# A decoder block on one core: values projected with channels on partitions, and the router's logits and the closing norm rearranged

## The chip, the cores and the metric

One Trainium2 chip, of which the kernel uses one core. The metric is the device time of one execution, in microseconds (us); less is better. The kernel before takes 1893.37 us, the median of three runs (1891.93 to 1896.53).

## The reference, cut to what matters

The block is one decoder layer for 512 tokens of width 2048, in fp32:

```python
h    = rmsnorm(x) * (1 + sc_a) + sh_a
proj = h @ w_in                       # q_a k_a v_a | q_b k_b v_b f_b
o_a  = sliding_window_gqa(q_a, k_a, v_a)          # 16 query heads, 4 kv heads
o_b  = forgetting_attention(q_b, k_b, v_b, f_b)   # 16 heads of 64: v_b is 512 x 1024
x    = x + g_a * (concat(rmsnorm(o_a), rmsnorm(o_b)) @ w_out)
h2   = rmsnorm(x) * (1 + sc_m) + sh_m
logits = h2 @ [w_group | w_expert] + bias         # 4 + 32 columns
# top 1 of 4 groups, then top 2 of its 8 experts, each a SwiGLU of 2048 -> 512 -> 2048
x    = x + g_m * moe(h2, logits)
out  = rmsnorm(x) * final_g
```

"The second head group" is `o_b`; its values are `v_b = h @ w_in[:, 3584:4608]`. The change touches how `v_b` is made, how the 36 logits are made, and the last `rmsnorm`.

## The kernel before

TensorE (PE) does nearly all of the arithmetic. A product `PE.matmul(o, lhsT, rhs)` keeps `lhsT` (128 rows, up to 128 columns) in the array and streams the columns of `rhs` past it; its result has the columns of `lhsT` on partitions. Projections split each factor into a rounded part and a rest and sum three products (`mm3`, lines 213 to 216). A plain fp32 product shows as two records in the trace.

The stages follow one another: the modulation and the first projections (to about 172 us), attention (to about 735), the output projection (to about 890), the routing, and 32 experts in 16 pairs (from about 900). The order on every queue is the order in which the program is written; nothing is reordered.

**Attention.** `attend` (line 844) walks over twelve segments (counted from 0), each some units of softmax work (`a1` scores and softmax, `b` transposes of the probabilities, two units later, `c` the product with the values). Between them a `Fill` hands PE pieces of the projections that later segments need. A piece states its own length in us when it yields; `fill.take(step)` lets pieces run until their stated lengths add up to what was granted, and a segment's end drains what is left before the next segment begins. `FILLS` (line 374) says which pieces lie in which segment: the values `v_b` are 4 groups of 256 columns (4 heads), 8 pieces each, and the last pieces of the groups end segments 1, 4, 7 and 9. Beside it, `side` steps sum up the modulation vectors on VectorE (DVE), ScalarE (ACT) and GpSimd (POOL).

A group of values is made by `natural` (line 539): the tokens' activations are the stationary factor, 256 columns of weights stream, and the result has tokens on partitions, as the product with the probabilities wants it. That is 3 products for each of 16 pieces of depth and 4 blocks of 128 tokens, 192 to a group, 768 in all. ACT copies the four blocks from PSUM into `vbs[g]` (line 903). Queries and keys are made by `transposed` (line 521) the other way: weights stationary, all 512 tokens streamed, channels on partitions.

**Output projection.** Its 2048 columns are made in four chunks of 512 (`cc` in the order 2, 0, 1, 3). While PE makes the next chunk, a `Tail` finishes the one before: for each block `tb` of 128 tokens it transposes the new `x1` (`tr`) and multiplies it with the router's weights (`logit`, line 1129): 4 products whose stationary factor is the transposed `x1`, with 36 streamed columns. DVE adds the 128x36 result into `lg` (lines 1134 and 1136). For the last chunk the four results stay in PSUM (`lp4`), are added to `lg` (line 1199) and multiplied by the tokens' `rs` (line 1211).

**Routing.** A chain of some 30 small DVE instructions chooses the experts. Meanwhile `turn(n)` gives PE `n` idle 128-column products: 22 before the ranks `rk` (line 1257), 8 behind them.

**Experts and the end.** Weights stream in through a ring of tiles; the DMA queue SP waits for a tile until PE is done with it. The last pair's output is made in five chunks of columns. As each is added to the total (line 1446), `last_norm` (line 1599) has ACT square it into `sf5`. Behind the last, DVE sums the five columns (1608), scales (1609) and takes the root (`rsqrt_`), and then writes 8 halves of the output, each followed by its transfer (1616 and 1617).

Of the kernel before, what the change touches and what calls it, by code (L numbers as in the profile page):

```python
# [8 lines left out]
F32 = mybir.dt.float32  # L9
# [3 lines left out]
AF = mybir.ActivationFunctionType  # L13
OP = mybir.AluOpType
AX = mybir.AxisListType

T = 512
D = 2048
TB = 4
EPS = 1e-6  # L20
# [33 lines left out]
def kernel(  # L54
# [8 lines left out]
    V, S, G, PE, SP = nc.vector, nc.scalar, nc.gpsimd, nc.tensor, nc.sync  # L63
# [23 lines left out]
    sb = att.enter_context(tc.tile_pool(name="start", bufs=1))  # L87
# [11 lines left out]
    ident = big.tile([128, 128], F32, name="ident")  # L99
# [113 lines left out]
    def mm3(o, lhi, llo, rhi, rlo, first, last, **kw):  # L213
        PE.matmul(o, lhi, rhi, start=first, stop=False, **kw)  # L214
        PE.matmul(o, lhi, rlo, start=False, stop=False, **kw)  # L215
        PE.matmul(o, llo, rhi, start=False, stop=last, **kw)  # L216

    hT_hi = fr.tile([128, 4, 4, T], F32R, tag="B", name="hT_hi")
    hT_lo = [big.tile([128, 4 * n, T], F32R, tag=f"C{i}", name=f"hT_lo{i}") for i, n in enumerate((3, 1))]

    def kt(ts, k, sl=slice(0, T)):

        return ts[k // 12][:, k % 12, sl]

    def proj_T(accs, hi, lo, cc, j, jj, o=0):

        for i, a in enumerate(accs):
            sl = slice(o + i * 128, o + (i + 1) * 128)
            mm3(a, hi[:, jj, sl], lo[:, jj, sl], hT_hi[:, cc, j, :], kt(hT_lo, 4 * cc + j),
                cc == 0 and j == 0, cc == 3 and j == 3)  # L230
# [158 lines left out]
    ws = Stream(items)  # L389
# [54 lines left out]
    sb = att.enter_context(tc.tile_pool(name="att", bufs=1, reuse_waits="tile"))  # L444
# [63 lines left out]
    def bank(shape, name):  # L508

        return pb["pool"].tile(shape, F32, tag=pb["tag"], name=name, bufs=pb["bufs"])  # L510
# [3 lines left out]
    def accs(tag, name):  # L514
        return [ps.tile([128, 512], F32, tag=tag, name=f"{name}{i}", bufs=2) for i in range(2)]
# [23 lines left out]
    def natural(w, banks, evac):  # L539

        per = 512 // w
        views = []

        def mm(q, hi, lo, tb, j):
            cc, k = q // 2, 2 * (q % 2) + j
            sl = slice(tb * 128, (tb + 1) * 128)
            mm3(views[tb], hT_hi[:, cc, k, sl], kt(hT_lo, 4 * cc + k, sl), hi[:, j], lo[:, j],
                q == 0 and j == 0 and tb % per == 0, q == 7 and j == 1 and tb % per == per - 1,
                skip_group_check=True)

        def piece_(q):
            if q == 0:
                b = banks()
                views.extend(b[tb // per][:, (tb % per) * w:(tb % per) * w + w] for tb in range(TB))
            hi, lo = ws.get()
            if q < 7:
                for j in range(2):
                    for tb in range(TB):
                        mm(q, hi, lo, tb, j)
                    yield w * 12 / 2400.0  # L560
            else:
                for tb in range(TB):
                    for j in range(2):
                        mm(q, hi, lo, tb, j)
                    if tb % per == per - 1:
                        for t in range(tb - per + 1, tb + 1):
                            evac(t, views[t])
                    yield w * 6 / 2400.0

        return [piece_(q) for q in range(8)]  # L570
# [107 lines left out]
    PB, PTB = 4, 2  # L678
# [209 lines left out]
    vbs = [sb.tile([128, TB, 256], F32, tag="vb", name=f"vb_{g}", bufs=2) for g in range(4)]  # L888
# [7 lines left out]
    def queries2(i):  # L896
        q = q_chunks(1, i)
        yield from transposed(f"qa{i}", [lambda acc, n=n: evac_q(acc, q[n]) for n in range(2)])

    VP = []  # L900
    for g in range(4):
        VP += natural(256, lambda g=g: accs("accv", f"vb{g}"),
                      lambda tb, o, g=g: S.activation(vbs[g][:, tb, :], o, AF.Copy))

    def fills(i):
        for kind, n, *to in FILLS[i]:
            if kind == "v":
                for v in VP[n:to[0]]:
                    yield from v
            else:  # L910
                yield from (queries2 if kind == "q" else heads2)(n)

# [83 lines left out]
    wrf = wr.rearrange("p c j e -> p (c j) e")  # L996
# [31 lines left out]
    total = lambda i: 2.56 * sum(to[0] - n if to else 8 for _, n, *to in FILLS[i])  # L1028
# [29 lines left out]
    ss2 = mo.tile([128, TB, 4], F32, name="ss2")  # L1058
    lg = mo.tile([128, TB, 36], F32, name="lg")

    def sm(shape, name, dt=F32):
        return mo.tile(shape, dt, name=name)

    def bc(t, shape):
        return t.to_broadcast(shape)
# [25 lines left out]
    class Tail:  # L1091
# [35 lines left out]
            S.activation(self.xT[tb], t, AF.Copy)  # L1127

        def logit(self, tb):
            lp = self.lp4[:, tb, :] if self.last else bank([128, 36], f"lp_{self.cc}_{tb}")  # L1130
            for j in range(4):
                PE.matmul(lp, self.xT[tb][:, j, :], wrf[:, self.cc * 4 + j, :], start=j == 0, stop=j == 3)
            if self.cc == 2:
                V.tensor_copy(lg[:, tb, :], lp)
            elif not self.last:
                V.tensor_add(lg[:, tb, :], lg[:, tb, :], lp)

        def steps(self):
            for tb in range(TB):
# [56 lines left out]
    tail.logit(2)  # L1196
    rms_x1()
    tail.logit(3)
    V.tensor_add(lg, lg, tail.lp4)
    pst.close()  # L1200
    frt.close()

# [5 lines left out]
    pb["pool"], pb["tag"], pb["bufs"], hold[0] = ps, "y", 4, True  # L1208
    while side_late:
        side_step()  # L1210
    V.tensor_mul(lg, lg, bc(rs[:, :, None], [128, TB, 36]))
    V.tensor_add(lg, lg, bc(brt[:, None, :], [128, TB, 36]))

    def one_hot(v, n, mx_, name):
# [11 lines left out]
    def turn(n):  # L1226

        for _ in range(n):
            PE.matmul(idle[:, :128], ident, ident, start=True, stop=True)

    turn(22)
    gl = lg[:, :, 0:4]
    gmax = sm([128, TB], "gmax")
    V.tensor_reduce(gmax, gl, axis=AX.X, op=OP.max)
# [20 lines left out]
    for tb in range(TB):  # L1255
        for k in range(tb + 1):
            PE.matmul(rk[:, tb, :], before if k == tb else ones_b, chosen_b[:, k].rearrange("p g e -> p (g e)"),
                      start=k == 0, stop=k == tb)
    turn(8)
    place = sm([128, TB, 4, 8], "place")  # L1260
    pf = place.rearrange("p t g e -> p t (g e)")
    V.scalar_tensor_tensor(place, chosen_b, FAR, bc(off.rearrange("p a b e -> p (a b) e")[:, None], [128, TB, 4, 8]),
# [251 lines left out]
    def total(tb):  # L1514

        if not x2s:
            x2s.extend(rp_.tile([128, D], F32, tag=f"x2{i}", name=f"x2_{i}") for i in range(TB))
        return x2s[tb]
# [80 lines left out]
    def last_norm(cols, tb=0):  # L1599
        if cols is None:  # L1600
            SP.dma_start(fg, bcast(final_g, D))
            return
        c0, c1 = cols
        i = CHUNKS.index(cols)
        S.activation(HID[:, :c1 - c0], total(tb)[:, c0:c1], AF.Square, accum_out=sf5[:, tb, i:i + 1])
        if c1 < D or tb < 3:
            return
        V.tensor_reduce(sf, sf5, axis=AX.X, op=OP.add)
        V.tensor_scalar(sf, sf, 1.0 / D, EPS, op0=OP.mult, op1=OP.add)
        rsqrt_(rf, sf, tf)  # L1610
        for tb in range(TB):
            y = ring_tile()
            for h in range(2):
                sl = slice(h * 1024, (h + 1) * 1024)
                yv = flat(y)[:, sl]
                V.scalar_tensor_tensor(yv, total(tb)[:, sl], rf[:, tb:tb + 1], fg[:, sl], op0=OP.mult, op1=OP.mult)
                SP.dma_start(out[tb * 128:(tb + 1) * 128, sl], yv)
# [113 lines left out]
```

## Time and profile before

| what | value |
|---|---|
| median of 3 runs | 1893.37 us |
| the profiled execution | 1895.8 us |
| its span, first to last instruction | 1893.9 us |
| PE busy | 1810.1 us, 96% |
| DVE, ACT, POOL busy | 1018.6, 748.7, 288.2 us |
| granted TensorE clock, mean share of full | 0.981 |
| moved from HBM | 567.82 MB read, 302 GB/s over the span |
| the chain that ended last | PE 74%, DMA 8%, ACT 7%, DVE 7%, issue 3%, POOL 1% |

The span and what lies around it (1.9 us) make the profiled execution's time, which is 2.4 us over the median. A busy PE counts from a product's start to its modelled end, so closely following products overlap. The granted clock is 1.00 at 2.4 GHz and 0.50 at 1.2 GHz.

### The profile page before, as it was taken

The numbers are of one execution on the slowest core, as the hardware profiler recorded it, in microseconds if no ns is written. First come the engines' busy times: TensorE is split into PE (matmuls) and PEld (weight loads), VectorE is DVE, ScalarE is ACT, GpSimd is POOL, SyncE is SP. The second block draws the span as 40 slices with busy tenths as digits, with TensorE's granted clock in tenths as the row PEclk, the third lists the DMA queues.
The fourth block names the chain that finished last, engine by engine and source line by source line (L and its number), as shares of the span: only waits on it lengthen the run. The fifth ranks groups of instructions, "written<-read, shape, count | busy, mean of one in ns | idle before, by whom it ended". The sixth has DMA issues, their size and how long they took to land.

```text
span 1893.9 us, 26581 instructions
## 1 busy us (share of the span) xinstructions
PE 1810.1 (96%) x10045; PEld 1131.1 (60%) x10045; DVE 1018.6 (54%) x1812; ACT 748.7 (40%) x1462; POOL 288.2 (15%) x217
## 2 busy tenths in 40 slices
PE   7998999899899999999999999999999999999995
PEld 5668887787787777778544454444444444444432
DVE  4334676666566545757555454544554545545435
ACT  3235656565555443345523233232322323323213
POOL 0000434443354321445000000000000000000000
PEclk8998999999999999999999999999999999999998
DMA  9984555565566342668989999999999999999995
GB/s 338 352 274 106 169 164 152 165 196 173 160 186 186 113 142 78 208 214 295 369 344 397 420 419 421 421 420 420 420 418 421 416 420 420 419 420 416 420 413 215
DMA packets 208791, 573.84 MB, mean 303 GB/s; under 512 B 22624, under 2 KB 110728, under 8 KB 159888
## 3 DMA queue, kind: packets, MB, share of 16 engines
q1 hardware_dynamic: 207744, 572.00, 80.3%
q8 instruction: 81, 1.33, 0.3%
q14 instruction: 54, 0.44, 0.1%
q10 hardware_dynamic: 912, 0.07, 0.0%
HBM read 567.82 MB, written 4.19 MB: 302 GB/s over the span
## 4 chain that ended last, share of the span: by engine, by line
PE 74%; DMA 8%; ACT 7%; DVE 7%; issue 3%; POOL 1%; SPq 0%; DVEq 0%; ACTq 0%; POOLq 0%
PE pu L1363 12%; PE pg L1363 11%; PE y L1385 9%; PE xe L1499 7%; PE o L1407 5%; DMA w<-in_w_up_dram 4%; PE qp L214 3%; PE qp L216 3%; PE qp L215 3%; DMA raw<-in_w_ada_dram 2%; PE gv L325 2%; PE acc L214 1%; PE acc L215 1%; PE acc L216 1%; PE ob L826 1%
## 5 line engine op out<-in xcount | busy, mean ns | idle before, releaser
L1363 PE MATMUL pu<-w,cw 128*64 128x512 f32 x1024 | 239.3, 593 | 4.7 <-DMA w<-in_w_up_dram 4.7
L1363 PE MATMUL pg<-w,cw 128*64 128x512 f32 x1024 | 235.5, 598 | 1.3 <-ACT cw L1508 0.8
L1508 ACT ACTIVATE cw<-xe,shM,scM 128x128 f32<-128x128 f32 x128 | 58.5, 458 | 429.2 <-PE xe L1499 396.2
L1385 PE MATMUL y<-w,more_f 128*64 128x512 f32 x960 | 214.2, 598 | 4.1 <-ACT xp_whi L1480 2.3
L1506 DVE TENSOR_SCALAR cw<-xe,scM,shM 128x128 f32<-128x128 f32 x128 | 52.4, 410 | 299.3 <-ACT cw L1508 299.3
L624 POOL TENSOR_TENSOR gb<-gb,raw 128x512 f32<-128x512 f32 x112 | 162.1, 1448 | 275.8 <-ACT raw L623 211.4
L1410 DVE SCALAR_TENSOR_TENSOR x<-o,wpair,x 128x512 f32<-128x512 f32 x240 | 163.2, 743 | 19.3 <-PE o L1407 19.3
L1363 PEld LDWEIGHTS pu<-w,cw 128*64 128x64 f32 x1024 | 76.0, 137 | 154.1 <-issue 140.3
L1480 ACT ACTIVATE xp_whi<-x,rs 128x256 fp32r<-128x256 f32 x236 | 162.6, 762 | 0.9 <-DVE rs L134 0.9
L1385 PEld LDWEIGHTS y<-w,more_f 128*64 128x64 f32 x960 | 71.2, 137 | 134.4 <-issue 111.1
L1363 PEld LDWEIGHTS pg<-w,cw 128*64 128x64 f32 x1024 | 69.7, 136 | 133.5 <-issue 128.4
L176 DVE TENSOR_TENSOR wlo_s<-raw,whi_s 128x512 fp32r<-128x512 f32 x96 | 91.4, 953 | 107.7 <-ACT whi_s L175 107.6
L1486 DVE SCALAR_TENSOR_TENSOR xp_wlo<-x,rs,xp_whi 128x256 fp32r<-128x256 f32 x232 | 144.8, 681 | 2.2 <-ACT xp_whi L1480 2.2
L621 DVE SCALAR_TENSOR_TENSOR ga<-raw,csil,ga 128x512 f32<-128x512 f32 x112 | 111.3, 994 | 26.2 <-DMA raw<-in_w_ada_dram 25.6
L1499 PE MATMUL xe<-cr,xp_whi 128*128 128x256 f32 x472 | 120.5, 294 | 0.0
L1499 PEld LDWEIGHTS xe<-cr,xp_whi 128*128 128x128 f32 x472 | 88.7, 188 | 47.3 <-issue 45.4
L1499 PE MATMUL xe<-cr,xp_wlo 128*128 128x256 f32 x472 | 114.3, 281 | 0.0
L214 PE MATMUL qp<-hT_hi,whi_s 128*128 128x512 f32 x256 | 107.3, 419 | 0.0
L216 PE MATMUL qp<-hT_hi,wlo_s 128*128 128x512 f32 x256 | 101.2, 395 | 0.0
L215 PE MATMUL qp<-hT_lo,whi_s 128*128 128x512 f32 x256 | 101.2, 395 | 0.0
L623 ACT ACTIVATE raw<-raw,csil 128x512 f32<-128x512 f32 x112 | 79.8, 713 | 34.0 <-DMA raw<-in_w_ada_dram 32.7
L1499 PEld LDWEIGHTS xe<-cr,xp_wlo 128*128 128x128 f32 x472 | 88.9, 188 | 0.0
(445 smaller groups left out, 3372.5 us busy)
## 6 DMA issues: line engine op xcount, KB each, us to landing
w<-in_w_gate_dram SPq DMA_DIRECT2D x128, 1024.0 KB, 10.6
w<-in_w_up_dram SPq DMA_DIRECT2D x128, 1024.0 KB, 13.9
w<-in_w_down_dram SPq DMA_DIRECT2D x126, 1024.0 KB, 10.3
raw<-in_w_ada_dram SPq DMA_DIRECT2D x128, 512.0 KB, 4.2
raws<-in_w_ada_dram SPq DMA_DIRECT2D x64, 512.0 KB, 8.9
raw<-in_w_in_dram SPq DMA_DIRECT2D x160, 128.0 KB, 2.8
raw<-in_w_out_dram SPq DMA_DIRECT2D x32, 512.0 KB, 3.8
raw<-in_w_in_dram SPq DMA_DIRECT2D x48, 256.0 KB, 3.3
```

Of the source, the lines that this page charges most:

```text
L214: PE.matmul(o, lhi, rhi, start=first, stop=False, **kw)
L215: PE.matmul(o, lhi, rlo, start=False, stop=False, **kw)
L216: PE.matmul(o, llo, rhi, start=False, stop=last, **kw)
L621: V.scalar_tensor_tensor(a, ts[n][:, j, :], s, a, op0=OP.mult, op1=OP.add)
L624: G.tensor_add(a, a, ts[n][:, j, :])
L1363: PE.matmul(o[64 * e:64 * e + 64, :], self.xe(cc)[:, j, 64 * e:64 * e + 64], w[cc, e][:, j, :], start=cc == 0 and j == 0, stop=cc == 3 and ...
L1385: PE.matmul(ys[dc][64 * e:64 * e + 64, :], HT[:, k, 64 * e:64 * e + 64], self.wd[k, e][:, dc, :], start=k == 0, stop=k == 3)
L1407: PE.matmul(o, self.ohT[:, tb, :], v, start=i == 0, stop=i == 1)
L1410: V.scalar_tensor_tensor(x2, o, self.w_col(tb), x2 if self.n else x1[dc][:, tb, :], op0=OP.mult, op1=OP.add)
L1480: S.activation(hi[tb], xv, AF.Identity, scale=s)
L1486: V.scalar_tensor_tensor(lo[tb], xv, s, hi[tb].bitcast(F32), op0=OP.mult, op1=OP.subtract)
L1499: PE.matmul(t[:, j, :], v[tb][:, j, :], OHS[:, tb].rearrange("p q s -> p (q s)"), start=tb + i == 0, stop=tb + i == TB)
```

## The change

The values are made by a new function `values`, with weights stationary and channels on partitions as queries and keys are. Each of a group's two banks is copied by ACT into an SBUF tile `vT` (of the ring `P`, four tiles, which also holds the softmax's probabilities), turned back by 4 transposes on PE into a PSUM tile, and copied by ACT into `vbs[g]`. The stated lengths of the pieces of a group go from 20.48 to 21.8 us; the grants stay.

The logits of the first three chunks are made with the 36 router columns stationary and 128 tokens streamed, in two halves of the array side by side (`e` 0 and 64). DVE adds the two 36x128 halves into `lgT`. In the last chunk a product with `both` (two stacked identities) brings `lgT` back into `lp4`, so that line 1199's addition goes and the multiplication by `rs` reads PSUM. `turn(22)` and `turn(8)` become `turn(15)` and `turn(6)`.

At the end, DVE squares the last chunk of the last two token blocks itself, POOL sums the first four columns of `sf5` ahead of time, and the last output block is written in three parts, not two.

```diff
+    def values(g):
+        banks = accs("accv", f"vb{g}")
+        vT = []
+        def piece_(q):
+            hi, lo = ws.get()
+            if q < 7:
+                for j in range(2):
+                    proj_T(banks, hi, lo, q // 2, 2 * (q % 2) + j, j)
+                    yield 1.3
+                return
+            for i in range(2):
+                for j in range(2):
+                    sl = slice(i * 128, (i + 1) * 128)
+                    mm3(banks[i], hi[:, j, sl], lo[:, j, sl], hT_hi[:, 3, 2 + j, :], kt(hT_lo, 14 + j), False, j == 1)
+                vT.append(sb.tile([128, T], F32, tag="P", name=f"vT_{g}_{i}", bufs=PB))
+                S.activation(vT[i], banks[i], AF.Copy)
+                yield 1.3
+            for i in range(2):
+                t = bank([128, TB, 128], f"vt_{g}_{i}")
+                for tb in range(TB):
+                    PE.transpose(t[:, tb, :], vT[i][:, tb * 128:(tb + 1) * 128], ident)
+                S.activation(vbs[g][:, :, i * 128:(i + 1) * 128], t, AF.Copy)
+                yield 0.5
+        return [piece_(q) for q in range(8)]
...
-        VP += natural(256, lambda g=g: accs("accv", f"vb{g}"),
-                      lambda tb, o, g=g: S.activation(vbs[g][:, tb, :], o, AF.Copy))
+        VP.append(lambda g=g: values(g))
...
+    lgT = mo.tile([128, T], F32, name="lgT")
+    G.memset(lgT, 0.0)
+    both = mo.tile([128, 36], F32, name="both")
+    G.memset(both, 0.0)
+    for e in (0, 64):
+        G.tensor_copy(both[e:e + 36, :], ident[e:e + 36, e:e + 36])
...
-            lp = self.lp4[:, tb, :] if self.last else bank([128, 36], f"lp_{self.cc}_{tb}")
+            if self.last:
+                lp = self.lp4[:, tb, :]
+                PE.matmul(lp, lgT[:, sl], both, start=True, stop=False)
+                for j in range(4):
+                    PE.matmul(lp, self.xT[tb][:, j, :], wrf[:, self.cc * 4 + j, :], start=False, stop=j == 3)
+                return
+            lp = bank([128, 128], f"lp_{self.cc}_{tb}")
             for j in range(4):
-                PE.matmul(lp, self.xT[tb][:, j, :], wrf[:, self.cc * 4 + j, :], start=j == 0, stop=j == 3)
-            if self.cc == 2:
-                V.tensor_copy(lg[:, tb, :], lp)
-            elif not self.last:
-                V.tensor_add(lg[:, tb, :], lg[:, tb, :], lp)
+                e = 64 * (j % 2)
+                PE.matmul(lp[e:e + 36, :], wrf[:, self.cc * 4 + j, :], self.xT[tb][:, j, :], start=j < 2, stop=j > 1)
+            for e in (0, 64):
+                o = lgT[e:e + 36, sl]
+                if self.cc == 2:
+                    V.tensor_copy(o, lp[e:e + 36, :])
+                else:
+                    V.tensor_add(o, o, lp[e:e + 36, :])
...
-    V.tensor_add(lg, lg, tail.lp4)
+    V.tensor_mul(lg, tail.lp4, bc(rs[:, :, None], [128, TB, 36]))
...
-    V.tensor_mul(lg, lg, bc(rs[:, :, None], [128, TB, 36]))
...
-    turn(22)
+    turn(15)
...
-    turn(8)
+    turn(6)
...
-        S.activation(HID[:, :c1 - c0], total(tb)[:, c0:c1], AF.Square, accum_out=sf5[:, tb, i:i + 1])
+        v = total(tb)[:, c0:c1]
+        if c1 == D and tb > 1:
+            V.tensor_tensor_reduce(YT[1][:, :c1 - c0], v, v, scale=1.0,
+                                   scalar=0.0, op0=OP.mult, op1=OP.add, accum_out=sf5[:, tb, i:i + 1])
+        else:
+            S.activation(HID[:, :c1 - c0], v, AF.Square, accum_out=sf5[:, tb, i:i + 1])
+        if i == 3 and tb == 3:
+            for k in range(1, 4):
+                G.tensor_add(sf, sf5[:, :, 0] if k == 1 else sf, sf5[:, :, k])
+            G.tensor_scalar(sf, sf, 1.0 / D, EPS, op0=OP.mult, op1=OP.add)
...
-        V.tensor_reduce(sf, sf5, axis=AX.X, op=OP.add)
-        V.tensor_scalar(sf, sf, 1.0 / D, EPS, op0=OP.mult, op1=OP.add)
+        V.scalar_tensor_tensor(sf, sf5[:, :, 4], 1.0 / D, sf, op0=OP.mult, op1=OP.add)
...
-            for h in range(2):
-                sl = slice(h * 1024, (h + 1) * 1024)
+            for c0, c1 in ((0, 1024), (1024, 2048)) if tb < 3 else ((0, 1024), (1024, 1664), (1664, 2048)):
+                sl = slice(c0, c1)
```

## Rows read from the trace of the kernel before

**Rows 1.** Windows by stage: engines' busy us (instructions), granted clock, DMA share, GB/s.

```profile
core 0: us, PE busy (x) PEld busy (x) DVE busy (x) ACT busy (x) POOL busy (x), PEclk, DMA share, GB/s
770.00:880.00 110.00, 103.95 (x509) 84.39 (x508) 69.44 (x78) 47.92 (x80) 60.49 (x39) 1.00 0.70 234
...
1100.00:1400.00 300.00, 297.70 (x1490) 142.16 (x1488) 153.24 (x257) 93.49 (x156) 0.00 (x0) 1.00 1.01 420
```

**Rows 2.** Timeline of PE: start us, length us; first and last of two unbroken series.

```profile
200.88 0.28 PE L215 MATMUL vb<-wlo_s,hT_hi 128*128 128x256 f32 x1
...
202.06 0.28 PE L216 MATMUL vb<-whi_s,hT_lo 128*128 128x256 f32 x1
...
393.44 0.39 PE L214 MATMUL qp<-hT_hi,whi_s 128*128 128x512 f32 x1
...
399.98 0.40 PE L215 MATMUL qp<-hT_lo,whi_s 128*128 128x512 f32 x1
```

**Rows 3.** Chain of waits: start us, us on the chain, engine, tile, line.

```profile
589.55 0.87 PE rb L687 x16
...
872.82 0.81 PE lp L1132 x8
...
876.49 0.48 PE x1T L1123 x4
```

**Rows 4.** Timeline of PE and ACT where groups 0, 1 and 2 of values end.

```profile
247.37 0.28 PE L216 MATMUL vb<-whi_s,hT_lo 128*128 128x256 f32 x1
...
250.25 0.63 ACT L903 ACTIVATE vb<-vb 128x256 f32<-128x256 f32 x2
250.78 0.48 ACT L754 ACTIVATE pta<-ta 128x384 f32<-128x384 f32 x1
...
391.71 0.28 PE L216 MATMUL vb<-whi_s,hT_lo 128*128 128x256 f32 x1
...
391.87 0.63 ACT L903 ACTIVATE vb<-vb 128x256 f32<-128x256 f32 x2
...
526.74 0.28 PE L216 MATMUL vb<-whi_s,hT_lo 128*128 128x256 f32 x1
...
527.62 0.64 ACT L903 ACTIVATE vb<-vb 128x256 f32<-128x256 f32 x2
...
622.21 0.62 ACT L788 ACTIVATE bb<-bp 128x512 f32<-128x512 f32 x1
```

**Rows 5.** Timeline of DVE: additions from PSUM of 36 and of 144 elements.

```profile
878.83 0.19 DVE L1136 TENSOR_TENSOR lg<-lg,lp 128x36 f32<-128x36 f32 x1 [1.79 <-PE lp L1132]
...
890.86 0.30 DVE L1199 TENSOR_TENSOR lg<-lg,lp 128x144 f32<-128x144 f32 x1 [0.28 <-PE lp L1132]
```

**Rows 6.** Timeline of PE around the routing; in brackets idle us before, and its releaser.

```profile
888.84 1.98 PE L1132 MATMUL lp<-wr,x1Ts 128*128 128x36 f32 x16
...
892.46 5.07 PE L1229 MATMUL idle<-ident 128*128 128x128 f32 x44
897.91 0.19 PE L1257 MATMUL rk<-chosen_b,before 128*128 128x32 bf16 x1 [0.38 <-DVE chosen_b L1253]
```

**Rows 7.** Timeline of the end on ACT and DVE.

```profile
1869.24 3.22 DVE L1446 SCALAR_TENSOR_TENSOR x<-o,wpair,x 128x256 f32<-128x256 f32 x8
...
1874.23 0.19 ACT L1605 ACTIVATION_READ_ACCUMULATOR cw<-x 128x1 f32 x1
...
1874.86 0.20 ACT L130 ACTIVATE tf<-sf 128x4 f32<-128x4 f32 x1 [0.44 <-DVE sf L1609]
```

**Rows 8.** Groups of POOL by shape: count, busy us, mean ns, idle us before.

```profile
L1484 POOL TENSOR_TENSOR xp_wlo<-cw,xp_whi 128x256 fp32r<-128x256 f32 x4 | 3.0, 747 | 11.0 <-ACT cw L1483 11.0
...
L1072 POOL IOTA down<- 128x8 f32 x1 | 0.1, 144 | 0.0
```

**Rows 9.** Windows: a stretch behind the last DVE instruction.

```profile
1887.00:1888.00 1.00, 0.00 (x0) 0.00 (x0) 0.00 (x0) 0.00 (x0) 0.00 (x0) 0.50 1.04 410
```

**Rows 10.** Timeline of PE: a long idle time in the attention.

```profile
517.95 1.54 PE L826 MATMUL ob<-ptb,vb 128*64 128x256 f32 x6 [3.29 <-ACT ptb L816]
```

**Rows 11.** Windows: the stretch that begins in that idle time.

```profile
516.60:523.30 6.70, 5.35 (x24) 4.63 (x25) 3.52 (x7) 4.33 (x10) 1.86 (x2) 0.50 0.31 80
```

More of the change, by code (lines that the diff above doesn't have):

```diff
@@ L907, in fills @@
             if kind == "v":
-                for v in VP[n:to[0]]:
-                    yield from v
+                for k in range(n, to[0]):
+                    if k % 8 == 0:
+                        VP[k // 8] = VP[k // 8]()
+                    yield from VP[k // 8][k % 8]
             else:
@@ L1129, in logit @@
         def logit(self, tb):
-            lp = self.lp4[:, tb, :] if self.last else bank([128, 36], f"lp_{self.cc}_{tb}")
-            for j in range(4):
-                PE.matmul(lp, self.xT[tb][:, j, :], wrf[:, self.cc * 4 + j, :], start=j == 0, stop=j == 3)
-            if self.cc == 2:
-                V.tensor_copy(lg[:, tb, :], lp)
-            elif not self.last:
-                V.tensor_add(lg[:, tb, :], lg[:, tb, :], lp)
+            sl = slice(tb * 128, (tb + 1) * 128)
+            if self.last:
[5 more added lines that the diff above has]
+            lp = bank([128, 128], f"lp_{self.cc}_{tb}")
+            for j in range(4):
+                e = 64 * (j % 2)
[6 more added lines that the diff above has]
+                    V.tensor_add(o, o, lp[e:e + 36, :])
         def steps(self):
```

## The prediction

> **What bounds the kernel now.** The windows by stage come first, since the shares of the whole span mix two limits. From about 900 us on the experts' weights stream: PE is busy 297.7 of 300 us and the transfers fill their engines [rows 1]. Nothing changed lies there, and the stream asks for its next tile when PE is done with one, so a start that is later or earlier by some us moves the whole stage by as much. The end of the span follows one chain behind the last weights. So three stretches decide: the attention with its fills, the output projection up to the routing, and the closing norm. In the output projection PE is busy 104 of 110 us, DVE 69, ACT 48, POOL 60 [rows 1]: PE is the nearest to a limit, but not alone. For the attention I then read the timeline of PE and ACT where each group of values ends [rows 4], since there the change puts a new dependency.
>
> **Values, PE's own work.** Series without a break give the spacing of products. Of 256 columns, 11 products start within 202.06 - 200.88 = 1.18 us, 0.118 each; of 512 columns, 29 within 399.98 - 393.44 = 6.54 us, 0.234 each [rows 2]. So 768 x 0.118 = 90.6 us become 384 x 0.234 = 89.9: -0.7. Added are 8 transposes to each of 4 groups; four take 0.48 us [rows 3], so 32 take 3.8. Net +3.1 us, of which little can hide, as PE is the busiest engine of the stage.
>
> **Values, the round trip.** Until now a group ended with ACT's copies, and PE went straight on. Now PE's next instructions are transposes of what ACT has copied, in a queue that nothing overtakes, and the segment's remaining fill is drained at its end, so no other piece stands between. I put the new instructions on the old timeline. A copy of 128x512 from PSUM takes 0.62 us [rows 4].
>
> Group 0 ends segment 1. PE's last product starts at 247.37 and the next could start at 247.49. ACT is behind: it reaches the first copy at 250.25, after a softmax that itself waited for DVE [rows 4]. The grants of this segment put the first copy ahead of the `pta` copy and the second behind it. So the first `vT` is there at 250.87; its transposes end at 251.35; `pta` (0.48) and the second copy end near 251.95, and the last transposes at 252.4. Of 4.9 us, 0.96 are the transposes counted above: 3.9 us of standing.
>
> Groups 1, 2 and 3 end segments 4, 7 and 9, which begin with an extra grant of 1.3 us; there both banks' products come before the `b` step and the two copies stand one behind the other. Group 1: PE free at 391.83, ACT at 391.87, second copy done at 393.1, end at 393.6, less 0.96: 0.8 us. Group 2: PE free at 526.86, ACT at 527.62, end 529.35: 1.5 us. Group 3 repeats group 1 within 0.1 us: 0.8. Sum 7.0 us.
>
> Behind the waiting transposes stand PE's score products of the next segment and the first pieces of its queries and keys; DVE's softmax and then ACT's exponentials wait for these. Bounds: nothing, if the time comes back at PE's later waits for ACT or DVE, and 7.0 + 4 x 0.6 = 9.4 if the next score product waits too, for a PSUM buffer that ACT must empty of the turned values. Those later waits mostly follow PE's own products of queries and keys, so they move along; I take 6.0. The `vT` tiles take two of the softmax's four `P` tiles for that time; what would be late is DVE's next softmax, whose scores come behind the same transposes, so I cost it at nothing, and at 0.5 us a group without that cover, inside the bounds. ACT's copies grow from 8 pairs of 0.63 to 16 of 0.62, +4.9 us; ACT is the least loaded of PE, DVE and ACT, and apart from the round trip this hides in its idle time, at worst 4.9.
>
> **Logits.** A block's logit takes PE 0.81 us in 8 records [rows 3]. No row shows 36 columns stationary in two halves; the nearest are the `rb` products, 64-column halves with 128 streamed columns: 16 records in 0.87 us, so 8 in 0.44. Twelve blocks save 12 x 0.37 = 4.4 us; if the halves don't run side by side, 8 records take 0.87 and 0.7 us are lost. DVE does two additions for one. 36 elements take 0.19, 144 take 0.30 [rows 5], so 128 about 0.28, two 0.56, +0.37 for a block and +4.4 in all. DVE stands in front of PE here too: the same queue splits the weights that PE waits for and sums the modulation whose tiles the weights' loads need. I count half of PE's saving (-2.2) and a quarter of DVE's addition (+1.1): -1.1, with ends -4.4 and +4.4 + 0.7 = +5.1. POOL's fills of `lgT` and `both` hide in its 50 idle us of this stage; uncovered they are under four operations of 0.75 [rows 8], 3 us.
>
> **Last chunk and routing.** Sixteen records take 1.98 us [rows 6], so the added product is 2 of about 0.1: 0.2 for each of four blocks. Two lie in the chain of the last chunk, +0.4. The other two delay `lp4` by up to 0.4; the addition that goes was 0.34 from start to start, so this pair is nothing. Bounds 0 to +0.8.
>
> **Idle products.** 44 records end at 892.46 + 5.07 = 897.53 and `rk` follows at 897.91, 0.38 later, on DVE [rows 6]. PE waits for DVE, so fewer idle products gain nothing there; behind `rk`, two fewer are 4 x 0.115 = 0.46 at most, in front of a gather that itself waits for DVE's one-hot rows. I take 0. What it may cost is a rival below.
>
> **The end.** ACT is the chain: its last four squares, 0.54 apart, end at 1874.42, and the root begins at 1874.86 [rows 7]. With the last two on DVE, ACT ends at 1873.34. DVE's additions end at 1872.46 [rows 7]; two squares of the additions' length (0.40) between and behind them put it at about 1873.3. POOL begins when ACT has squared the fourth chunk, 4 x 0.54 before 1874.42, at 1872.26, with four operations in a row on 4 elements. The nearest rows are 0.144 for 8 elements and 0.747 for 256 [rows 8]; with a pause each I take 0.27, near the small one: 1873.35. One DVE instruction (0.2) then stands for two: the root begins near 1873.7, -1.1 us; at 0.75 each POOL ends at 1875.3 and +0.7 is lost. I take -1.0. The third part of the last block gains nothing: the transfers still run at 410 GB/s more than a us after DVE's last write [rows 9], so they bound it.
>
> **Sum.** +3.1 + 6.0 - 1.1 + 0.4 + 0 - 1.0 = +7.4 us. The profiled execution took 1895.8 (span 1893.9 and 1.9 around it): 1903.2. It stands 2.4 over the median of the runs, 1893.4; against that the forecast is 1900.8. A measurement of this kernel can tell about 0.3% from no change, 5.7 us: below 1887.7 is faster, above 1899.1 slower.
>
> **Rivals.**
> *The round trips come back.* One mechanism: PE loses its lead over ACT at a group's end, and finds at its next waits that ACT and DVE are done. For it: PE does have such waits, 3.29 us at one place [rows 10]. Against: that one ends on copies of keys which PE itself has just made. With 1.0 in place of 6.0 the sum is +2.4: 1895.8. It decides if less than half of the 7.0 stays.
> *The logits pay in full.* The output projection follows PE alone, DVE's additions hide, and the round trips are hidden as well: +3.1 - 4.4 + 0.4 - 1.1 = -2.0, 1891.4. For it: PE is 95% busy there; against: DVE 63% and in one queue with the splits.
> *The clock falls.* With 15 idle products PE is done at 892.46 + 5.07 x 15/22 = 895.9 and stands 2.0 us before `rk`. Behind an idle time of 3.29 us [rows 10] the granted clock was 0.50, 1.2 GHz, for 6.7 us [rows 11]. If it fell here, the first 32 gathering products at 0.118 would take 3.8 us more, of which some 0.8 is slack: +3.0, 1903.8. The Trainium skill (TensorE: Matmul & The Clock Gate, PE-mode transpose) adds that transposes don't count as work for the clock; by that rule group 0's 4.9 us is one idle time, and by [rows 10, 11] a fall behind it costs about 2 us more, 1902.8. No row here shows a stretch of transposes alone.
>
> **How the numbers follow.** Round trips stay: 0.48, own range 1897 to 1906. They come back: 0.28. Logits in full: 0.14. Clock: 0.10. The range reaches from 1889, the end of the third, to 1907, the clock on top of PSUM waits. Slower gets 0.40 of the first case and 0.08 of the fourth, faster 0.10 from the third with its bounds, the rest, 0.42, is no change.
>
> **What would show it.** In the trace after: idle times of PE of about 4, 1, 1.5 and 1 us in front of the transposes of `vT`, released by ACT's copy; logits of about 0.45 us; DVE's pairs of 0.28; the root about 1.1 us nearer to the last addition; granted clock 1.00 through the gather. Wrong would be: no idle time there, or attention ending as early as before in spite of it.

## The result

The changed kernel took 1910.64 us (median of 4 runs, 1908.12 to 1912.03), the kernel before 1893.28 beside it: ratio 1.0085, interval 1.0065 to 1.0106. It is slower by about 17 us, where the forecast was 1900.8 (at most 1907). The sign was right, the size was not.

### The profile after

Its stages as windows: the attention (here from the first product of the values to the first of `op`, a product of the output projection), the output projection in two parts (to the first logit, and from there to the first idle product), the experts (first gate product to last product). Columns as in [rows 1].

```profile
173.20:684.10 510.90, 475.96 (x2598) 369.02 (x2596) 301.25 (x610) 289.54 (x659) 195.96 (x136) 0.95 0.54 159
684.10:804.40 120.30, 119.39 (x584) 93.74 (x584) 63.19 (x99) 44.92 (x76) 29.79 (x30) 0.97 0.36 119
804.40:918.40 114.00, 108.23 (x553) 83.28 (x553) 78.07 (x106) 51.24 (x90) 58.06 (x40) 0.99 0.71 243
929.90:1888.40 958.50, 949.88 (x4733) 442.27 (x4732) 483.65 (x819) 294.81 (x504) 0.41 (x2) 1.00 0.99 411
```

The same in the kernel before:

```profile
172.70:657.20 484.50, 460.77 (x2950) 379.28 (x2948) 306.70 (x610) 284.17 (x659) 193.64 (x136) 0.97 0.56 168
657.20:777.20 120.00, 119.10 (x584) 93.86 (x585) 63.22 (x99) 44.80 (x76) 28.60 (x26) 0.97 0.37 123
777.20:892.50 115.30, 108.82 (x546) 88.27 (x546) 74.16 (x94) 51.21 (x89) 60.63 (x40) 1.00 0.69 232
904.30:1871.70 967.40, 954.35 (x4733) 445.35 (x4732) 483.45 (x819) 294.60 (x504) 0.00 (x0) 1.00 0.99 407
```

Attention is 26.4 us longer, the output projection 1.0 us shorter, the experts' stage 8.9 us *shorter*, though no line of it was changed. The first and the last are to be explained.

PE's idle time in front of the turn (the transposes that turn the values back), from the groups of the attention, and the timeline at the end of groups 0 and 3:

```profile
L922 PE MATMUL vt<-ident,vT 128*128 128x128 f32 x32 | 6.9, 364 | 10.7 <-ACT vT L917 10.7
```

```profile
246.94 0.40 PE L216 MATMUL vb<-hT_hi,wlo_s 128*128 128x512 f32 x1
249.97 1.97 PE L922 MATMUL vt<-ident,vT 128*128 128x128 f32 x8 [2.64 <-ACT vT L917]
...
642.67 1.07 PE L922 MATMUL vt<-ident,vT 128*128 128x128 f32 x4 [3.09 <-ACT vT L917]
644.49 1.12 PE L922 MATMUL vt<-ident,vT 128*128 128x128 f32 x4 [0.75 <-ACT vT L917]
```

The mean of a transpose, 364 ns, is the second sign: in the kernel before, the softmax's transposes of 128 columns took 282. Windows over the stretches with reduced clock in the attention show why: the column behind POOL's is the granted clock, 0.50 of full speed, 1.2 of 2.4 GHz.

```profile
250.23:260.47 10.24, 10.24 (x39) 8.93 (x38) 6.07 (x13) 4.18 (x10) 5.68 (x5) 0.50 0.58 166
345.80:356.04 10.24, 7.93 (x28) 5.79 (x29) 4.99 (x10) 5.04 (x13) 6.86 (x5) 0.50 0.32 87
437.96:441.37 3.41, 3.41 (x11) 2.53 (x9) 2.12 (x5) 1.24 (x5) 1.51 (x1) 0.50 0.82 233
492.57:495.98 3.41, 3.41 (x12) 2.72 (x11) 1.56 (x6) 2.42 (x5) 0.00 (x0) 0.50 0.72 216
...
543.77:547.18 3.41, 3.41 (x11) 2.83 (x10) 0.56 (x1) 2.82 (x6) 1.28 (x1) 0.50 0.41 137
584.74:588.15 3.41, 3.41 (x12) 1.76 (x13) 3.04 (x5) 1.35 (x4) 1.77 (x1) 0.50 0.32 79
642.76:649.59 6.83, 6.08 (x19) 4.63 (x20) 2.21 (x5) 3.69 (x7) 2.55 (x2) 0.50 0.30 79
680.31:690.55 10.24, 8.20 (x22) 5.56 (x22) 7.53 (x11) 4.84 (x8) 6.36 (x4) 0.50 0.17 41
```

Ten such stretches touch the attention (the last begins shortly before its end), 55.1 us of it; before, five, 24.7 us. A product at half clock takes twice its time at full clock, so half of the time that PE works there is lost. That gives a split of the attention for every run (us; "at half" is PE's busy time in those stretches, of which half is lost; "work" is length - idle - half of "at half", PE's work as it would be at full clock):

```
                        length   idle   at half   work
before                   484.5   23.5     19.7    451.2
after                    511.0   34.8     49.7    451.3
e1  old values           482.5   23.1     16.8    451.0
e2  values alone         509.7   36.3     42.2    452.3
e3  turn of other data   501.8   35.3     27.3    452.9
e4  kept busy            502.9   28.4     21.8    463.6
e12 standing alone       497.7   33.7     22.4    452.8
e13 turn by products     510.4   39.0     30.7    456.1
e14 standing, transposes 502.4   32.6     29.8    454.9
```

Before to after: idle +11.3, half clock +15.0 (half of 30.0), work +0.1: the 26.4 us. "At half" is not a fixed quantity: over the ten profiles with the old values and no added standing it lay between 8.8 and 19.7 us. Differences of a few us in it mean nothing. "Half-clock time" in the expectations below is the length of the stretches themselves, with PE's idle time in them: 55.1 us after, 24.7 before.

A logit on the chain of waits (start, us, count), to be held against [rows 3]; then, from the timelines, DVE's pair behind a logit, the routing and the end; last, the window around the routing, with the granted clock:

```profile
898.47 0.56 PE lp L1176 x8
```

```profile
844.83 0.58 DVE L1182 TENSOR_TENSOR lgT<-lgT,lp 36x128 f32<-36x128 f32 x2 [1.91 <-PE lp L1176]
...
918.42 3.51 PE L1274 MATMUL idle<-ident 128*128 128x128 f32 x30
923.53 0.19 PE L1302 MATMUL rk<-chosen_b,before 128*128 128x32 bf16 x1 [1.60 <-DVE chosen_b L1298]
...
1889.10 0.20 POOL L1659 TENSOR_TENSOR sf<-sf,sf 128x4 f32<-128x4 f32 x1 [1.96 <-ACT cw L1655]
1889.39 0.20 POOL L1660 TENSOR_SCALAR sf<-sf 128x4 f32<-128x4 f32 x1
...
1889.15 0.48 DVE L1491 SCALAR_TENSOR_TENSOR x<-o,wpair,x 128x256 f32<-128x256 f32 x1
1890.24 0.16 DVE L1663 SCALAR_TENSOR_TENSOR sf<-sf,sf 128x4 f32<-128x4 f32 x1
...
1890.43 0.20 ACT L130 ACTIVATE tf<-sf 128x4 f32<-128x4 f32 x1 [0.39 <-DVE sf L1663]
```

```profile
905.00:930.00 25.00, 22.54 (x166) 19.74 (x167) 19.93 (x52) 16.18 (x30) 6.10 (x7) 1.00 0.86 350
```

### The profile page after: what moved, and what is told of

The parts are those of the page before. It is cut to its first block, busy times and chain, and to the rows that moved or that the text cites. A ratio compares the mean times of both kernels' runs of the same rounds, so it can differ in the third digit from the quotient of the medians.

```text
span 1910.3 us, 25913 instructions
## 1 busy us (share of the span) xinstructions
PE 1818.5 (95%) x9683; PEld 1109.6 (58%) x9683; DVE 1017.8 (53%) x1827; ACT 753.2 (39%) x1458; POOL 289.7 (15%) x225
## 4 chain that ended last, share of the span: by engine, by line
PE 74%; ACT 7%; DVE 7%; DMA 7%; issue 3%; POOL 1%; SPq 1%; ACTq 0%; DVEq 0%; POOLq 0%
PE pu L1408 12%; PE pg L1408 11%; PE y L1430 9%; PE xe L1544 7%; PE o L1452 5%; DMA w<-in_w_up_dram 4%; PE qp L214 3%; PE qp L216 3%; PE qp L215 3%; DMA raw<-in_w_ada_dram 2%; PE gv L325 1%; PE acc L214 1%; PE ob L826 1%; DMA raws<-in_w_ada_dram 1%; PE acc L215 1%
## 5 line engine op out<-in xcount | busy, mean ns | idle before, releaser
L176 DVE TENSOR_TENSOR wlo_s<-raw,whi_s 128x512 fp32r<-128x512 f32 x96 | 86.0, 897 | 102.7 <-ACT whi_s L175 102.1
L621 DVE SCALAR_TENSOR_TENSOR ga<-raw,csil,ga 128x512 f32<-128x512 f32 x112 | 105.7, 943 | 16.5 <-DMA raw<-in_w_ada_dram 15.6
```

The lines of the kernel that those rows point to most:

```text
L621: V.scalar_tensor_tensor(a, ts[n][:, j, :], s, a, op0=OP.mult, op1=OP.add)
```

## The experiments

Theory A: PE's standing in front of the turn is lost, and the clock that falls behind it costs as much again. Rivals: the new form of the work lowers the clock (C); the standing comes back later (D); other edits carry part of the loss (B). The experts' 9 us needed theories of their own.

### e1 and e2: the change in two halves

e2 is the kernel before with the same lines the other way round.

```diff
 e1
-VP.append(lambda g=g: values(g))
+VP += natural(256, lambda g=g: accs("accv", f"vb{g}"),
+              lambda tb, o, g=g: S.activation(vbs[g][:, tb, :], o, AF.Copy))
```

> The changed kernel with the values made as before (rows of tokens on partitions, no turn, no vT); logits, idle products and closing norm as changed. Theory A (the values carry the whole loss: idle times in front of the turn, +11.3 us, and products at half the granted clock, +15.0 us): attention is as long as before (first output-projection product about 484.5 us after the first product of the values, half-clock time about 25 us in it), the rest gains 1 to 2 us: 1891.5 us, ratio to before 0.999, to the change 0.990. Theory B (a part of the loss is that of the other edits, by code or weights that come later): 1896 us or more. A third reading concerns the experts' stage, which the changed kernel ran 7.3 us faster than before in one profile (892.8 against 900.1 us from first gate product to last pair): if that comes from the edits outside the values it stays here (1884 us), if it comes from the later start or is spread of single runs it is not here.

> The kernel before with the values alone changed. Theory A: attention is 26 us longer as in the changed kernel; whether the experts' stage gives 7 to 9 us back again tells whether that belongs to the values (later start of the stream) or to the other edits. With the give-back 1912 us (ratio to before 1.010), without it 1919 (1.0135). Theory B: less than 1908.

Measured: e1 1882.96 us, ratio 0.9946 (0.9930 to 0.9963); e2 1920.76, ratio 1.0147 (1.0130 to 1.0164). The values alone cost 28 us, 27 of them in the attention against e1's. e1 has the short experts' stage (957.1 us), e2 the long one (966.9), so the gain goes with the other edits and not with a later start. B falls: no loss shows outside the values.

### e3 and e4: without the wait, and without the standing

```diff
 e3
-PE.transpose(t[:, tb, :], vT[i][:, tb * 128:(tb + 1) * 128], ident)
+PE.transpose(t[:, tb, :], ident, ident)
 e4, BUSY = ((11, 0), (6, 0), (8, 3), (13, 3))
+for _ in range(BUSY[g][i]):
+    PE.matmul(t[:, 0, :], ident, ident, start=True, stop=True)
```

> The changed kernel, but the 32 transposes of the turn read the identity and not vT, so they wait for no copy of ACT; the second head group's values are left wrong, every instruction stays. Theory A (the standing in front of the turn, 10.7 us, is itself lost and brings the half clock behind it): both go, attention shortens by 10.7 + most of the 15 us: 22 to 26 us, and with a full-length experts' stage 1890 to 1896 us. Rival C (the half clock comes from the new form of the work, fewer and longer products and the transposes, whatever stands): only the 10.7 us go, half-clock time in the attention stays near 55 us: about 1900. Rival D (the time lost in front of the turn comes back at other waits): idle time of PE in the attention stays over 30 us.

> The changed kernel with products of identity by identity (into the bank that the turn then overwrites) in the places where PE stands in front of the turn: 11, 6, 8+3 and 13+3 of them at 0.23 us, about as long as the idle times measured there (2.6, 1.6, 1.95+0.75, 3.1+0.75 us). The wait for ACT stays, only PE doesn't stand. Theory A with the clock as the larger part: the half-clock time in the attention falls from 55 to about 25 us, PE's products get 15 us back, less what the products overshoot (1 to 2 us): 1896 to 1899 us. Rival C (the form of the work sets the clock): half-clock time stays, 1910 to 1912 us.

e3's total (3335.08 us) can't be compared: with wrong values its experts' stage takes 2378 us, presumably because the tokens go to other experts. Its attention can. The wait in front of the turn is gone, yet PE's idle time stays at 35.3 us:

```profile
L786 PE MATMUL bp<-cumT,pick 128*128 128x512 f32 x14 | 6.9, 492 | 7.8 <-ACT ptb L816 5.2 <-DVE ptb L818 2.6
...
L661 PE MATMUL cps<-zf,tri 128*128 128x16 f32 x8 | 1.5, 265 | 1.7 <-ACT pta L754 1.7
```

In the changed kernel `bp` waits 2.6 us, `cps` not at all. PE runs on to the next thing that ACT must do, a PSUM bank to be emptied (`bp` reads no `ptb`), and stands there: ACT's lateness is what PE meets, the turn only where it meets it. D is right in this form (the standing moves), not in the form that time comes back. PE's time at half clock fell from 49.7 to 27.3 us with as much idle time as in the changed kernel: it is not the sum of the idle time that sets it. A expected the idle time to go, C the clock to stay, and both were wrong there; that the stage is 9.2 us shorter (501.8 us) is the clock's doing alone.

e4 took 1903.56 us, ratio 1.0055 (1.0039 to 1.0072), above the 1896 to 1899 expected. Its attention has 21.8 us at half clock in place of 49.7 (half-clock time 24.7 us, as A expected): 14.0 us back, and the idle time fell by 6.4. But its 44 added products cost 12.3 us of work, twice the idle time that they took away. That the clock followed the standing, with turn and new form unchanged, speaks against C as the whole cause.

### e12, e14, e13: standing and transposes apart

e12 is e1 with one product per group that reads ACT's last copy; in e14 it is eight transposes. e13 is the changed kernel with the turn as ordinary products.

```diff
 e12, behind each group's last piece
+t = bank([128, 128], f"st_{g}")
+PE.matmul(t, vbs[g][:, 3, 0:128], ident, start=True, stop=True)
 e14, in place of that product
+for k in range(8):
+    PE.transpose(t[:, k % 4, :], vbs[g][:, 3, 0:128], ident)
 e13
-PE.transpose(t[:, tb, :], vT[i][:, tb * 128:(tb + 1) * 128], ident)
+PE.matmul(t[:, tb, :], vT[i][:, tb * 128:(tb + 1) * 128], ident, start=True, stop=True)
```

> As e1_rest (values in the old way, no turn), and behind each group's last piece one product of PE that reads the copy ACT makes last: PE stands at the four group ends for ACT's copies, without a transpose and without the new form of the products. Theory A (standing at these places brings the half clock): idle time of PE in the attention 8 to 13 us more than e1's 23.1, half-clock time from 21 to 40 us or more, total 1883.0 + 8 to 13 + 8 to 15 = 1899 to 1911 us. Rival C (the half clock needs the transposes or the 512-column products): half-clock time stays near 21 to 25 us, 1891 to 1896 us. Rival D (the standing comes back at later waits): 1883 to 1887 us.

> As e12_stand (values in the old way, PE waits at each group's end for ACT's last copy), but eight transposes of that copy behind the wait instead of one product: the standing and the transposes of the change without the new form of the products. 32 transposes cost 3.8 us of PE, less the 4 products' 0.9: 2.9. Theory T: half-clock time rises from e12's 29 to 40 us or more, 1906 to 1912 us. Theory S: it stays near 29, 1902 us.

> The changed kernel with the 32 transposes of the turn made as ordinary products with the identity (the same result, two passes for one, so 32 x 0.12 = 3.8 us more work on PE). The standing in front of them is kept. Theory T (transposes behind a standing time don't hold the clock up): half-clock time in the attention falls from 55 to 35 us or less, 10 us come back, 3.8 are spent: 1902 to 1906 us. Theory S (the length and places of the standing decide, whatever instruction follows): half-clock time stays at 45 us or more: 1911 to 1915 us.

Measured: e12 1899.33 us, ratio 1.0028 (1.0017 to 1.0039), against e1's 0.9946 about 15.5 us more; e14 1903.20, 1.0046 (1.0030 to 1.0062); e13 1909.05, 1.0080 (1.0054 to 1.0107). The standing in e12, all four groups together and, from the timeline, group 2:

```profile
L903 PE MATMUL st<-ident,vb 128*128 128x128 f32 x8 | 2.3, 370 | 10.2 <-ACT vb L908 10.2
...
537.82 0.49 PE L903 MATMUL st<-ident,vb 128*128 128x128 f32 x2 [3.35 <-ACT vb L908]
```

Four products that wait, in the kernel with the old values, make 15 us: idle +10.6, half clock +2.8, work +1.8. So standing at these places is lost in full and doesn't come back. The clock's part is smaller than A expected: 22.4 us at half clock for e1's 16.8, half-clock time 28.9 us for the 40 or more expected. Nor does the clock fall behind every standing: behind group 2's 3.35 us (second row) the granted clock was 1.00 up to 621 us, and in the changed kernel behind group 1's 1.58 us too.

Eight transposes in each place (e14) bring the time at half clock to 29.8, with 3.9 us more in total, of which 2.1 are work. Products in place of the transposes (e13) bring the change's 42 to 50 (e2 and after) down to 30.7, but cost 4 to 5 us of work and 4 of idle time, and end within the interval of the changed kernel. In half-clock time both come close to theory T (36.3 us in e14 for "40 or more", 35.5 in e13 for "35 or less"), in total time they lie nearer to S. e3 points to T as well: there PE stood in front of products and not of transposes, and had less time at half clock. The rule of the Trainium skill (TensorE: Matmul & The Clock Gate, PE-mode transpose) that transposes don't count as busy in the same way is not refuted. With the scatter of "at half" these runs can't fix the transposes' share, which stays open, between nothing and some 10 us.

Nor is C out of it. Of the 12.7 us of clock that e2 has over e1, half of 42.2 - 16.8, the standing alone brings 2.8 (e12) and the transposes 3.7 more (e14); the other 6.2 come only with the new form, and each of the three is within the scatter or near it. With the new form PE stands at two places away from the turn, 2.6 us in front of a `bp` (1.5 before) and 2.4 in front of a product of the values (nothing before). The clock fell behind both in the changed kernel (492.57, 584.74), and also in e3 (482.81, 574.97) and e4 (486.28, 578.44), where PE stood at most 1.5 us in all in front of the turn. So the clock's 15 us come from where PE stands, in front of the turn and elsewhere, and how much each cause takes is not shown.

### The experts' 9 us: e5 to e11, e15

The two new tiles `lgT` and `both` take 2208 bytes of each partition in the pool `mo`. Four tiles of the ring that the experts' weights are written to lie behind them, half of those used once the stream is under way; the others lie in the pool `wring`. All of these runs are the kernel before, or e1, with a tile that only shifts others (in brackets its columns of 4 bytes); e15 also lays the small tile `v1` into the bytes of another to make room:

```diff
 e5 (8), e6 (16), e9 (40), e10 (552), e11 (40) in the kernel before; e8 (8) in e1
+pad = mo.tile([128, 8], F32, name="pad")
+G.memset(pad, 0.0)
 e7 (8), e15 (56) in e1, e11 (56): at the end of wring
+padr = rp_.tile([128, 8], F32, name="padr")
+G.memset(padr, 0.0)
```

> The kernel before, and nothing else but a tile of 32 bytes per partition (set to zero by POOL) in the pool `mo` in front of `rs`, where the change has its two new tiles (2048 and 160 bytes). Four of the weights' ring tiles lie behind it in this pool: their addresses were 32 bytes past a multiple of 64 before, are multiples of 64 in the change and here; the other ring tiles stay where they were. Theory P (place): the weights' transfers run faster into such tiles, steady rate 424 GB/s for 420, experts' stage 958 us for 967 from the first gate product to the last: 1884.5 us, ratio 0.9955. Theory E (the edits themselves, idle products, logits or the closing norm, bring the experts' 9 us): 1893, ratio 1.000, 967 us.

> The same with a tile of 64 bytes: the ring tiles of `mo` move too, but stay 32 bytes past a multiple of 64. Theory P: as before, 1893 us, 967 us from the first gate product to the last. If any shift of the tiles does it: 1884.5. Theory E: 1893.

> The changed kernel with the values made as before (as e1_rest), and a tile of 32 bytes at the end of the right-hand pool `wring`, which moves the other eight ring tiles to multiples of 64 as well. Theory P: the steady rate rises again, by at most as much as the first step gave: between 1874 and 1882 us against 1883.0; if the ring is by then bound by the products and not by the transfers, 1881 to 1883. Theory E: 1883, no change.

> As e1_rest, and a tile of 32 bytes in `mo` in front of the two new ones, which puts the ring tiles of `mo` back to 32 bytes past a multiple of 64. It leaves the logits, idle products and closing norm alone. Theory P: what they give by themselves, 1 to 2 us: 1891.5 us (ratio to before 0.999), experts' stage 967 us. Theory E: 1883, 958 us.

> The kernel before with a tile of 160 bytes in `mo`: the ring tiles of that pool then begin at multiples of 256 (128256), as in the changed kernel (130304), but almost 2 KB lower. The 32 and 64 bytes tried left them 128 and 160 past one, with no gain. Theory M (what counts is the place of `mo`'s tiles to a multiple of 256): 958 us from the first gate product to the last, 424 GB/s, 1884.5 us, ratio 0.9955. Theory N (the place must be that of the changed kernel, or one of the edits is needed beside it): 1893, 967 us.

> The kernel before with a tile of 2208 bytes in `mo`: every later tile of that pool has the address that it has in the changed kernel, and no edit is in it. Theories M and N's first half (place alone): 958 us, 1884.5. If an edit is needed beside the place: 967 us, 1893.

> As e9, and a tile of 224 bytes at the end of `wring`, so that all twelve ring tiles begin at multiples of 256. Theory M: at least e9's time, 1884.5; the third and fourth ring tiles of `wring`, whose transfers were still slow in e1 and e7, run as the others and give up to 4 us more: 1880 to 1884.5. Theory N: 1893.

> The version that the runs point to: logits, idle products and closing norm as changed, values as before, all twelve ring tiles of the weights at multiples of 256 (a tile of 224 bytes at the end of `wring`; `v1` laid into `emul`'s bytes makes the room). If the place of the ring and the edits add up: e1's 1883.0 less what e11 gained over e9 (about 5 us in the experts' stage): 1877 to 1880 us, ratio to before 0.992. If the edits bring nothing beside the place: e11's time, 1880.6.

Bytes past a multiple of 256 at which the ring's tiles begin, the experts' stage, and the ratio:

```
              mo  wring   stage us   time us   ratio (interval)
before        96    224     967.1
e5 pad 32    128    224     968.2    1894.23   1.0002 (0.9990 to 1.0014)
e6 pad 64    160    224     966.9    1893.50   0.9999 (0.9986 to 1.0012)
e8 e1+32      32    224     969.8    1893.69   0.9995 (0.9982 to 1.0008)
e1             0    224     957.1    1882.96   0.9946 (0.9930 to 0.9963)
e7 e1, wring   0    192     957.9    1881.18   0.9933 (0.9913 to 0.9954)
e9 pad 160     0    224     958.6    1887.21   0.9960 (0.9946 to 0.9974)
e10 pad 2208   0    224     959.8    1885.36   0.9956 (0.9941 to 0.9972)
e11 both       0      0     953.5    1880.56   0.9935 (0.9912 to 0.9958)
e15 e1, both   0      0     956.0    1880.46   0.9924 (0.9902 to 0.9946)
```

My first form of the theory (multiples of 64) fell with e5, which had expected 1884.5; multiples of 256 held in e9, without any edit and at another address. In the window of [rows 1] the rate is 420 GB/s before, and in e5, e8, e9 and e11:

```profile
1100.00:1400.00 300.00, 297.82 (x1490) 141.59 (x1488) 153.32 (x257) 93.46 (x156) 0.00 (x0) 1.00 1.01 419
```

```profile
1100.00:1400.00 300.00, 297.28 (x1487) 141.87 (x1488) 154.27 (x257) 93.42 (x156) 0.00 (x0) 1.00 1.01 418
```

```profile
1100.00:1400.00 300.00, 298.63 (x1498) 140.47 (x1495) 154.35 (x257) 93.64 (x156) 0.00 (x0) 1.00 1.01 423
```

```profile
1100.00:1400.00 300.00, 298.93 (x1506) 143.24 (x1505) 154.97 (x259) 94.24 (x159) 0.00 (x0) 1.00 1.01 426
```

The rates differ by about one per cent, and 9 us are one per cent of the stage: it follows these transfers, whose share of their engines is 1.01 in all four. e8 gives the remaining edits by themselves: ratio 0.9995, -0.9 us, anywhere from -3.4 to +1.5. e15 and e11 beat both kernels, and equally: with the ring in place, logits, idle products and closing norm show no gain that these runs can tell.

## Why the prediction was wrong

- **Values, PE's own work**: +3.1 predicted, +0.1 measured (+1.1 in e2). The transposes took the time that was predicted, 4.1 us for 3.8. But the products became cheaper by 3.3 us (2.5 in e2) and not by 0.7: counted from each start to the next product, and half of it at half clock, the 768 took 97.1 us and the 384 take 93.8. Both spacings from [rows 2], taken from unbroken series, were too low, the 0.118 the more so.
- **Round trips**: 6.0 taken of 7.0; measured 10.7 in front of the turn, 11.3 in all. Group 0 stood less than the 3.9 predicted (2.64), the others more: 1.58 for 0.8, 2.70 for 1.5, 3.84 for 0.8. "Group 3 repeats group 1" is a sentence that failed. ACT's queue has the softmax ahead of the copy, and that waits for DVE (first row of ACT), which before it splits weights (`wlo_s`) and sums the modulation (`ga`):

```profile
636.57 1.42 DVE L176 TENSOR_TENSOR wlo_s<-raw,whi_s 128x512 fp32r<-128x512 f32 x1 [1.91 <-ACT whi_s L175]
637.92 1.77 DVE L621 SCALAR_TENSOR_TENSOR ga<-raw,csil,ga 128x512 f32<-128x512 f32 x1
...
640.80 0.72 ACT L801 ACTIVATE pb<-pb,nmb 128x512 f32<-128x512 f32 x1 [3.65 <-DVE nmb L799]
641.43 0.19 ACT L801 ACTIVATION_READ_ACCUMULATOR pb<-pb,nmb 128x1 f32 x1
641.52 0.61 ACT L175 ACTIVATE whi_s<-raw 128x512 fp32r<-128x512 f32 x1
642.04 0.57 ACT L917 ACTIVATE vT<-vb 128x512 f32<-128x512 f32 x1
643.84 0.60 ACT L917 ACTIVATE vT<-vb 128x512 f32<-128x512 f32 x1 [1.22 <-PE vt L922]
```

  The prediction had put the new steps on ACT's old timeline, where ACT was ready 0.04 us after PE at group 1 and 0.76 at group 2; here the first copy began 2.5 us after the end of PE's last product (639.58). The second copy did not follow the first, either: it began only behind PE's first four transposes (last row), which made PE stand 0.75 us more in groups 2 and 3. Why it waits for them isn't shown.
- **The clock** is the step that made the miss: the sum has it at nothing. It was a rival at 0.10, priced at 3.0 us at the gather or 2 at group 0 (by its own [rows 11], half of 5.35, it is 2.7). At the gather nothing fell: PE stood 1.60 us before `rk` for the 2.0 predicted, and the clock stayed at 1.00. In the attention it cost 15.0 us (11 to 13 in e2 against the old form). [Rows 10, 11] had shown one idle time and one fall; the new kernel has five more stretches, and others are longer. Two of the five are behind the turn (543.77, 642.76), as is the longer one at 250.23; three are behind idle times of 1.5 to 2.6 us elsewhere (437.96, 492.57, 584.74), of which the prediction had none. A fall should have stood in the sum, as a price times a chance, at every place where PE would stand; it came behind three of the four turns.
- **The round trips come back** (0.28): no. e12 shows such standing lost, e3 that a removed wait moves to the next bank.
- **Logits**: eight records take 0.56 us, for 0.81 before [rows 3]: 0.25 saved in place of 0.37, since the `rb` products, from which 0.44 was taken, were not near enough. DVE's pair took 0.58 (0.56 predicted).
- **The end**: POOL's operations took 0.20 each, 0.29 from start to start (0.27 taken); from the last product to the root 2.4 us, before 3.5: -1.1, as predicted. But from the root to the span's end it took 19.9 us for 19.1. SP now issues a ninth store, for the third part, which the prediction had costed at nothing: it took 0.90, most others 0.33. In e4, where it took 0.42, the stretch was 19.1 again. Little of the gain is left.
- Logits, last chunk, idle products and end together: -1.7 predicted, -0.9 in e8 with its interval.
- **"Nothing changed lies there"**, of the experts' stage: wrong by 9 us. A new tile moved the tiles behind it.

Values +28, place -8, the rest -1: with e2, e9 and e8 some 19, against 17 measured. That the forecast of +7.4 missed by 10 us and not by 18 is luck: the place of the ring, which it did not see, gave 8 back.

## What to carry to other kernels

Look twice before an instruction of the busiest engine goes directly behind a copy by another. What PE stood there was lost (e12), and behind three of the four places the clock fell and charged the next products too, so give both a price at every place. Removing the wait helps only if the engine that is late is late no longer: in e3 the next shared banks collected the same time. And when an edit allocates anything, look at the addresses of the tiles behind it: two tiles that only shifted a ring gained more here than all the logic around them.

## What the runs showed of the hardware

- Transfers of 8192 bytes to a partition ran faster when the tiles in `mo` began at multiples of 256 bytes: mean time of such a packet in the window of [rows 1] 314.8 ns before, 311.6 in e9, and 310.1 in e11, where those in `wring` do so too. Starts 32, 96, 128 and 160 bytes past a multiple (e8, before, e5, e6) gave 314.8 to 315.6. The Trainium skill (DMA: Bandwidth & Descriptors, How a descriptor splits into AXI transactions) says that the first transaction of a descriptor that doesn't start at such a multiple begins at the boundary below, and that the unused bytes in front cost beats. The boundary agrees; but the page speaks of bytes that are fetched, and the runs moved the place that is written. By an estimate from the page's beats, 1 more for a start 32 bytes past and 3 for 96, the one would cost a third of the other; the runs show no such grading.
- The same attention, instruction for instruction, spent between 8.8 and 19.7 us of PE's time at half clock in the ten kernels that share it: half of the difference, some 5 us, is the uncertainty of a single profile for this reason alone.
